# Writing out the order of the first up pairs, and three other buffers for the last pair's totals

## The chip, the cores and the metric

One NeuronCore of a Trainium2 chip runs the whole layer as one launch. The metric is the device time in microseconds (us) of one execution; the number compared is the median of several runs. Engines are named as in the profile: PE (TensorE matmul), PEld (its weight loads), DVE (VectorE), ACT (ScalarE), POOL (GpSimd), SP (the queue that issues most DMAs).

## The reference, cut to what matters

A hybrid layer on x (1024 tokens by 1024 channels, float32): a state-space branch and an attention branch, merged by gates, then a gated MLP with a causal convolution of three taps along the tokens. The change lies in the MLP:

```python
h = rms_norm(x, norm_ffn_g[i])
u = causal_depthwise_conv(h @ w_up[i], conv_ffn_w[i], conv_ffn_b[i])
u_gate, u_val = jnp.split(u, 2, axis=-1)
x = x + (jax.nn.silu(u_gate) * u_val) @ w_down[i]
```

`w_up` is 1024 by 5632, so `u_gate` and `u_val` have 2816 channels each, 22 tiles of 128.

## The kernel before, in words

**Numbers.** Each float32 operand is split into a high half (a cast on ACT to a rounded format) and a low half (operand minus high half, a subtraction on DVE or POOL). A product of two 128-wide blocks is three matmuls of 128x128 by 128x512, high by high, high by low, low by high (lines L175, L176, L177).

**Up pairs.** The MLP's first product goes over 22 pairs `q` (`q.j` = 0 to 21; q0, q1, q2, q3 are the first four). A pair is one gate tile and one value tile of `w_up` (raw weights `q.r1` and `q.r2`, tiles `ur1` and `ur2`) times the 1024 tokens. As a 2x2 block product (two halves of the 1024 inputs, two halves of the tokens) it is done in seven block products instead of eight, with sums of weights (`w_sums`) and sums of activations (the `job`s "t1" to "t4" and "22", whose high and low halves are tiles `tq` and `h`). A block product is 12 matmuls. PE does them per pair as: `p12` (two block products, banks `q.x` and `q.y`), `p5` (bank `q.z`), `p6` (onto `q.x`), `p3` (onto `q.z`), `p7` (onto `q.x`), `p4` (onto `q.x`). Operands: `q.a` (w_first), `q.b` (w_second), `q.c` (w_third), `q.d` (w_fourth), `q.e` for p4(q0). p5(q3) means p5 of the fourth pair.

**Between the products** a bank is copied out by ACT (L1315 `c11`, L1322 `p5`, L1327 `p6`, L1367 `c21`) or added into a row by DVE (L1316, L1338 `c22`, L1353 `p3`, L1473 and L1477 for the first two pairs). The next product onto the same bank has to wait for that reader. The rows `ug` (gate) and `uv` (value) hold 1024 tokens and two zeros in front. A conv half takes a new bank: one ACT start (L1346) and two DVE steps (L1348). `gate` puts the silu of both halves into `uc`; `value_half` multiplies the value conv into it on DVE (L1371); `totals` writes sums of two pairs to DRAM (`f_d`) for the down product, which has the same 7-of-8 form.

**Buffers.** PSUM has 8 banks: two named `lin`, six named `dps` (`bank6`), shared by products and convs, given out as the program is recorded; a new holder waits for the last reader of the old one. `wraw` has two buffers, `lt` three, `ur1` and `ur2` two each.

**Order.** PE's instructions are chained in the order of the code everywhere. The other engines (not SP) are chained in code order only in three stretches, one of them from `strict` to `strict_end`, which in the kernel before ends right behind p4(q1). Outside these a scheduler places instructions. From `ordered` on (the last pair, `totals` of both last pairs on DVE, first operands of the down product, L1559 and L1564) code order holds again.

Of the kernel before, what the change touches and what calls it, by code (L numbers as in the profile page):

```python
# [72 lines left out]
def tile_hybrid_layer(ctx: ExitStack, tc: tile.TileContext, x, cols, cons, w_main, w_small, w_uq, w_ukv,  # L73
# [105 lines left out]
    def act_tile():  # L179
        return hp.tile([P, 2, 512], F32R, name="h")  # L180
# [941 lines left out]
    def w_raw(q, name=None):  # L1122
        q.r1 = up.tile([P, KD, P], F32, name="ur1", bufs=2)
        q.r2 = up.tile([P, KD, P], F32, name="ur2", bufs=2)
        for raw, j in ((q.r1, q.j), (q.r2, FFT + q.j)):
            nc.sync.dma_start(out=raw, in_=w_up[j])
            if name:
                behind(name)

    def w_tiles(n, wide=True):  # L1130
        if n < 2:
            return wpool.tile([P, KD, P], F32R, name="whi"), wpool.tile([P, KD, P], F32R, name="wlo")
        k = KD if wide else 4
        return (ux[0].tile([P, k, P], F32R, name=f"xhi{n}", bufs=1), ux[0].tile([P, k, P], F32R, name=f"xlo{n}", bufs=1))

    def w_split(raw, hl, eng):
        hi, lo = [t[:, 0:raw.shape[1], :].rearrange(flat) for t in hl]
        r = raw.rearrange(flat)
        S.copy(hi, r)  # L1139
        eng.tensor_sub(lo, r, hi.bitcast(F32))  # L1140
        return hl

    def w_first(q):
        q.a = w_split(q.r1, w_tiles(0), G)

    def w_sums(q, t=None):
        q.s = t or up.tile([P, KD, P], F32, name="us", bufs=1)
        G.tensor_tensor(q.s[:, 0:4, :], q.r2[:, 0:4, :], q.r2[:, 4:8, :], op=ALU.add)
        G.tensor_tensor(q.s[:, 4:8, :], q.s[:, 0:4, :], q.r1[:, 0:4, :], op=ALU.subtract)
        G.tensor_tensor(q.r2[:, 0:4, :], q.r1[:, 0:4, :], q.r2[:, 0:4, :], op=ALU.subtract)  # L1150
        G.tensor_tensor(q.r1[:, 4:8, :], q.r1[:, 4:8, :], q.s[:, 4:8, :], op=ALU.subtract)
# [17 lines left out]
    with tc.tile_pool(name="ep", bufs=2) as ep:  # L1169
# [159 lines left out]
        def p7(q):  # L1329
            drain([product(q.x, q.c, 0, "t3", False, True)])  # L1330
# [6 lines left out]
            value_row(q)  # L1337
            V.tensor_tensor(q.uv[:, 514:1026], q.x, q.q, op=ALU.add)  # L1338

        def conv(q, kind, u, half):  # L1340

            c = bank6()
            ct = kind * FFT + q.j
            cw = CG_FW + 3 * ct
            n = half * 512
            S.activation(c, u[:, n + 2:n + 514], AF.Identity, bias=col(CG_FB + ct), scale=col(cw + 2))  # L1346
            for k in range(2):
                V.scalar_tensor_tensor(c, u[:, n + k:n + k + 512], col(cw + k), c, op0=ALU.mult, op1=ALU.add)  # L1348
            return c

        def p3(q):
            drain([product(q.z, q.d, 0, "22", False, True)])
            V.tensor_tensor(q.ug[:, 514:1026], q.z, q.s2, op=ALU.add)  # L1353

        def gate_tile_(q):
            q.gate = ux[0].tile([P, T], F32, name="uc0", bufs=2)

        def gate(q):
            gate_tile_(q)
            for half in range(2):  # L1360
                S.activation(q.gate[:, hs_(half)], conv(q, 0, q.ug, half), AF.Silu)
# [16 lines left out]
        def totals(q, eng=G):  # L1378
            kp = q.j // 2
            t0, t1 = q.gate[:, 0:512], q.gate[:, 512:1024]  # L1380

            def total(n, a, b, op, t):
                eng.tensor_tensor(t, a, b, op=op)  # L1383
# [34 lines left out]
        def low(left=0):  # L1418
            while len(late) > left:
                lo, v, hi, name, i, t = late.pop(0)  # L1420
                V.tensor_sub(lo, v, hi.bitcast(F32))
                BQ[name][i] = t

        def job(name, i, v, t, minuend=None, subtrahend=None):

            if minuend is not None:
                V.tensor_tensor(v, minuend, subtrahend, op=ALU.subtract)
            hi, lo = [t[:, n, :].rearrange("p (i c) -> p i c", c=P) for n in range(2)]
            S.copy(hi, v)
# [43 lines left out]
        V.tensor_tensor(q0.q, q0.x, q0.q, op=ALU.add)  # L1473
# [34 lines left out]
    def first_operands(k):
        a, b = [up.tile([P, KD, P], F32, name=f"ur{n}", bufs=2).rearrange(rows) for n in (1, 2)]
        nc.sync.dma_start(out=a, in_=f_d[k][:, 0:2, :].rearrange(rows))  # L1510
        nc.sync.dma_start(out=b, in_=w_down[0, k].rearrange(rows))
        first.append((split_pair(a, act_tile), split_pair(b, tq)))

    def raw_w(count=[0]):
        count[0] += 1
        return wpool.tile([P, 2, 512], F32, name=("whi", "wlo")[count[0] % 2])

    for j in range(3, FFT):
        nx = Pair()
        nx.j = j  # L1520
        w_raw(nx)
        w_first(nx)
        p5(q)
        if j == 3:
# [24 lines left out]
        before, q = q, nx
# [271 lines left out]
```

## Time and profile before

| | |
|---|---|
| runs, not profiled | 2189.15, 2190.39, 2189.43 us; median 2189.43 |
| profiled execution | 2194.85 us; its span (first to last instruction) 2192.9 us |
| mean granted PE clock | 0.996 |
| PE busy | 2144.1 us of the span |
| pairs 0 to 3 | p7(q0) starts at 1558.37, p12(q4) at 1617.28 us |
| a load of 512 KB (q2's value weights) | issued at 1560.59, used by POOL at 1564.15 us |
| last pair's end, start of the down product | PE's wait at 1984.7 to 1988.0 us |

Times in the prediction's rows are microseconds from the start of the span. A timeline row gives start, duration, engine, line, operation, what it writes from what, shape, count, and in brackets how long the engine stood idle before it and who released it. A row with x2 or x4 is a run of like instructions in one, so the step to the next row is the price of the run.

### The profile page before, as it was taken

The page shows a single profiled execution, that of the slowest core. Times are in us where ns is not written, and L with a number is a line of the kernel's source. Part 1 is how long each engine was busy: PE and PEld are TensorE (multiplying, and loading weights), DVE is VectorE, ACT ScalarE, POOL GpSimd, SP SyncE. Part 2 cuts the span into 40 slices and gives each one's busy share as a digit, 9 for nine tenths or more (in the row PEclk, how much of TensorE's full clock was granted, in tenths as well). Part 3 has the DMA queues.
Part 4 walks back from the last instruction along what each step waited for, and adds up shares of the span by engine and source line. Part 5 has one row for each costly group of instructions (what it writes and reads, how often), then busy time and mean ns, then how long its engine had stood idle before and what let it go on. Part 6 is the DMA issues. An engine that isn't in the chain of part 4 may idle for free. (4 is left out here: it accounts for less than half of the span.)

```text
span 2192.9 us, 30400 instructions
## 1 busy us (share of the span) xinstructions
PE 2144.1 (98%) x10844; PEld 1712.9 (78%) x10844; DVE 1447.2 (66%) x2609; ACT 1063.8 (49%) x2032; POOL 889.8 (41%) x1005
## 2 busy tenths in 40 slices
PE   8999999999999999999999999999899999999999
PEld 6877776777777887778877787887678888887887
DVE  4466656576664469898877745545766666676773
ACT  5445454555454446665654424324655545554341
POOL 2244424432443237665545311003277777840000
PEclk9999999999999999999999999999999999999999
DMA  4221111111112324554366566552133222248752
GB/s 148 69 69 46 40 54 62 49 38 55 64 44 78 108 77 148 180 168 154 116 220 208 173 215 222 162 174 97 61 107 106 102 101 96 106 156 305 268 188 82
DMA packets 121768, 269.50 MB, mean 123 GB/s; under 512 B 13520, under 2 KB 25744, under 8 KB 121616
## 3 DMA queue, kind: packets, MB, share of 16 engines
q1 hardware_dynamic: 105600, 214.99, 29.3%
q0 software_dynamic: 14528, 49.29, 6.8%
q10 hardware_dynamic: 1488, 3.28, 0.4%
q8 instruction: 85, 1.39, 0.3%
q14 instruction: 67, 0.55, 0.1%
HBM read 201.97 MB, written 65.54 MB: 122 GB/s over the span
## 5 line engine op out<-in xcount | busy, mean ns | idle before, releaser
L175 PE MATMUL lin<-h,whi 128*128 128x512 f32 x1440 | 591.6, 411 | 0.7 <-DVE lt L330 0.6
L177 PE MATMUL lin<-h,wlo 128*128 128x512 f32 x1440 | 563.7, 391 | 0.1
L176 PE MATMUL lin<-h,whi 128*128 128x512 f32 x1440 | 562.5, 391 | 0.0
L175 PEld LDWEIGHTS lin<-h,whi 128*128 128x128 f32 x1440 | 270.7, 188 | 83.5 <-issue 33.8
L177 PEld LDWEIGHTS lin<-h,wlo 128*128 128x128 f32 x1440 | 270.3, 188 | 60.0 <-DVE wlo L154 0.5
L176 PEld LDWEIGHTS lin<-h,whi 128*128 128x128 f32 x1440 | 271.4, 189 | 53.0 <-issue 6.7
L153 ACT CAST whi<-wraw 128x512 fp32r<-128x512 f32 x232 | 140.9, 619 | 256.8 <-PE lin L176 112.7
L154 POOL TENSOR_TENSOR wlo<-wraw,whi 128x512 fp32r<-128x512 f32 x134 | 193.3, 1460 | 169.0 <-ACT whi L153 165.1
L664 POOL TENSOR_TENSOR acc<-acc,e 128x512 f32<-128x512 f32 (+3 forms) x80 | 78.9, 987 | 246.0 <-ACT e L659 224.3
L659 ACT ACTIVATE e<-s 128x512 f32<-128x512 f32 (+1 forms) x192 | 93.4, 492 | 152.1 <-DVE s L657 131.1
L1140 DVE TENSOR_TENSOR xlo<-ur,xhi 128x512 fp32r<-128x512 f32 (+1 forms) x41 | 82.9, 2022 | 61.4 <-ACT xhi L1139 61.4
L154 DVE TENSOR_TENSOR wlo<-wraw,whi 128x512 fp32r<-128x512 f32 x98 | 69.9, 725 | 73.0 <-ACT whi L153 72.7
L850 ACT ACTIVATE seg<-abc,acum 128x128 f32<-128x128 f32 x256 | 80.1, 389 | 46.9 <-PE yp L891 37.3
L176 PE MATMUL dps<-tq,h 128*128 128x512 f32 x242 | 96.6, 399 | 3.1 <-DVE tq L1564 3.1
L177 PE MATMUL dps<-tq,h 128*128 128x512 f32 x242 | 96.4, 398 | 0.0
L175 PE MATMUL dps<-tq,h 128*128 128x512 f32 x242 | 96.3, 398 | 0.0
L812 DVE SCALAR_TENSOR_TENSOR xg<-craw,cl,xg 128x1024 f32<-128x1024 f32 x48 | 73.8, 1537 | 27.4 <-ACT xg L810 26.9
L664 DVE TENSOR_TENSOR acc<-acc,e 128x512 f32<-128x512 f32 (+3 forms) x80 | 55.3, 691 | 37.8 <-ACT e L659 37.2
L670 PE MATMUL pv<-e,vt 128*64 128x512 f32 (+3 forms) x384 | 72.9, 499 | 0.0
L629 DVE CUSTOM_DVE_ANT_0 s<-s,negw 128x128 f32<-128x128 f32 (+3 forms) x128 | 62.3, 495 | 13.5 <-PE s L627 13.3
L175 PE MATMUL s<-qh,kh 97*128 97x512 f32 (+1 forms) x192 | 68.6, 357 | 1.3 <-ACT qh L644 0.9
L1216 POOL DMA_DIRECT2D mt<-m_d x16 | 8.6, 540 | 145.6 <-DVE gt L1225 96.6
(628 smaller groups left out, 5133.4 us busy)
## 6 DMA issues: line engine op xcount, KB each, us to landing
wraw<-in_w_main SPq DMA_DIRECT2D x112, 256.0 KB
ur<-in_w_up SPq DMA_DIRECT2D x44, 512.0 KB
abc<-ac_d POOLq DMA_DIRECT2D x32, 512.0 KB, 5.4
wraw<-in_w_ssd SPq DMA_DIRECT2D x64, 256.0 KB
ar<-f_d SPq DMA_DIRECT2D x32, 512.0 KB
f_d<-wraw POOLq DMA_DIRECT2D x33, 256.0 KB, 2.4
g_d<-lt SPq DMA_DIRECT2D x32, 256.0 KB
z_d<-lt SPq DMA_DIRECT2D x32, 256.0 KB
```

The lines of the kernel that those rows point to most:

```text
L153: S.copy(hi, raw)
L154: (eng or V).tensor_sub(lo, raw, hi.bitcast(F32))
L175: PE.matmul(ps, lhsT=ah, rhs=bh, start=first, stop=False, **more)
L176: PE.matmul(ps, lhsT=ah, rhs=bl, start=False, stop=False, **more)
L177: PE.matmul(ps, lhsT=al, rhs=bh, start=False, stop=last, **more)
L629: V.tensor_tensor_reduce(ps[:, 0:w], ps[:, 0:w], negw[:, 512 - w:512], 1.0, 2 * NEG, ALU.add, ALU.max, nm[:, j, i:i + 1])
L659: S.activation(e[:, c0:512], ps[:, 0:w], AF.Exp)
L664: (V if hd else G).tensor_tensor(accs[hd][:, c0:512], accs[hd][:, c0:512], e[:, c0:512], op=ALU.add)
L670: PE.matmul(pv[hd * 64:(hd + 1) * 64, c0:512], lhsT=vt[:, j, hd * 64:(hd + 1) * 64], rhs=es[hd][:, c0:512], start=first, stop=last)
L812: V.scalar_tensor_tensor(c, raw[:, k:k + T], col(cw + k), c, op0=ALU.mult, op1=ALU.add)
L850: S.activation(seg[:, hd, :], abc[:, hd, :], AF.Relu, bias=acum[:, c, 8 * g + hd:8 * g + hd + 1], scale=-1.0)
L1140: eng.tensor_sub(lo, r, hi.bitcast(F32))
```

## The change

Three things. First, `strict_end` moves: code order now holds on all engines through p4 of the third pair (q2), and that stretch of code is written out by hand instead of by conditions `j == 3` in the loop. Second, within it: two of the "t3" jobs go ahead of p5's bank copy; the additions that read p7(q0)'s and p7(q1)'s bank come right behind those products; `w_sums(q2)` is done on DVE instead of POOL, its last two sums later; q2's raw gate weights go into q0's tile in two DMAs; the copy of q2's first bank (`s1`) and the casts of q2's and q3's weights come ahead of the silus; both gate halves of a pair get their ACT start and bank before either is finished (`conv_begin`, `conv_end`, `gate_both`). Third, the three totals of the last pair (`q.j == 21`) are formed in `lt` buffers instead of `wraw`.

The diff's core (names of new helpers; `successor` is `w_raw` and `w_first` of a new pair):

```diff
-        def conv(q, kind, u, half):
+        def conv_begin(q, kind, u, half):
             c = bank6()
...
+            return c, u, n, cw
+
+        def conv_end(c, u, n, cw):
             for k in range(2):
                 V.scalar_tensor_tensor(c, u[:, n + k:n + k + 512], col(cw + k), c, op0=ALU.mult, op1=ALU.add)
             return c
...
+        def gate_both(q):
+            gate_tile_(q)
+            begun = [conv_begin(q, 0, q.ug, half) for half in range(2)]
+            for half, c in enumerate(begun):
+                S.activation(q.gate[:, hs_(half)], conv_end(*c), AF.Silu)
...
             def raw():
+                if q.j == FFT - 1:
+                    return lt.tile([P, 512], F32, name="lt")
                 return wpool.tile([P, 512], F32, name="wraw", bufs=2)
...
-        for q in (q0, q1):
-
-            p5(q, q.ug[:, 514:1026])
-        for i in range(4):
+        def job_t3(i):
             job("t3", i, b[3, i], tq(), b[4, i], b[3, i])
+
+        for i in range(2):
+            job_t3(i)
+        p5(q0, q0.ug[:, 514:1026])
+        job_t3(2)
+        p5(q1, q1.ug[:, 514:1026])
+        job_t3(3)
...
         p6(q0)
-        q1.c = w_split(q1.r2, w_tiles(0), V)
-        for i in range(2):
-            job("t4", i, b[2, i], tq(), b[2, i], b[1, i])
+        q1.c = w_tiles(0)
+        S.copy(q1.c[0].rearrange(flat), q1.r2.rearrange(flat))
+        job_t4(0)
+        V.tensor_sub(q1.c[1].rearrange(flat), q1.r2.rearrange(flat), q1.c[0].rearrange(flat).bitcast(F32))
         p6(q1)
-        for i in range(2, 4):
-            job("t4", i, b[2, i], tq(), b[2, i], b[1, i])
+        for i in range(1, 3):
+            job_t4(i)
+        p7(q0)
+        V.tensor_tensor(q0.q, q0.x, q0.q, op=ALU.add)
+        job_t4(3)
         low()
         q0.e = w_split(q0.r2[:, 4:8, :], w_tiles(1), V)
-        p7(q0)
-        V.tensor_tensor(q0.q, q0.x, q0.q, op=ALU.add)
...
+    s1 = lt.tile([P, 512], F32, name="lt")
+    S.copy(s1, q2.x)
+    p3(q0)
     w_second(q2, V)
-    w_third(q2)
-    p3(q0)
-    gate(q0)
+    gate_tile_(q0)
+    begun = [conv_begin(q0, 0, q0.ug, half) for half in range(2)]
+    w_sums_last(q2, V)
     p3(q1)
     w_fourth(q2)
...
+    q, nx = q2, q3
+    p5(q)
+    gate_row(q)
+    V.tensor_tensor(q.ug[:, 2:514], q.y, s1, op=ALU.add)
+    value_half(q0, 0)
+    p6(q)
+    w_sums(nx)
+    p3(q)
+    value_half(q0, 1)
+    totals(q0)
+    w_second(nx)
+    p7(q)
+    c22(q)
+    gate_both(q1)
+    gate_row(nx)
+    drain([p12(nx)])
+    value(q1)
+    c11(nx)
+    w_fourth(nx)
+    p4(q)
+    c21(q)
+    gate_both(q)
+    w_third(nx)
+    strict_end = len(nc.cur_bb.bb.instructions)
+    value(q)
```

In the three places below, the line numbers are each kernel's own; the changed kernel's L1349, L1354, L1326, L1319 and L1398 are before's L1346, L1348, L1322, L1315 and L1383.

ACT behind p4(q1), before: `dps_14887` is q2's first bank (`q2.x`), `dps_15298` is p5(q2)'s bank, `uc0_15262` is q0's gate, `dps_15263` and `dps_15268` are its conv halves, `xhi2` and `xhi3` the high halves of q2.c and q2.d, `whi_15294` that of q3.a.

```order
L1361 ACT_TABLE_LOAD
L1361 ACTIVATE uc0_15262<-dps_15263 128x512
L1139 CAST whi_15241<-us_15228 128x1024
L1139 CAST xhi2_15245<-ur2_15225 128x1024
L1346 ACTIVATE dps_15268<-ug_14861,cl_80 128x512
L1139 CAST xhi3_15286<-ur1_15224 128x512
L1139 CAST whi_15294<-ur1_15290 128x1024
L1346 ACTIVATE dps_15337<-uv_15233,cl_80 128x512
L1346 ACTIVATE dps_15342<-uv_15233,cl_80 128x512
L1322 COPY lt_15311<-dps_15298 128x512
L1361 ACTIVATE uc0_15262<-dps_15268 128x512
L1315 COPY lt_15315<-dps_14887 128x512
```

The same place now; `lt_15239` is the copy of q2's first bank, `dps_15300` p5(q2)'s bank, `uc0_15258` q0's gate, `whi_15289` q3.a.

```order
L1521 COPY lt_15239<-dps_14887 128x512
L1139 CAST whi_15254<-us_15228 128x1024
L1349 ACTIVATE dps_15259<-ug_14861,cl_80 128x512
L1349 ACTIVATE dps_15261<-ug_14861,cl_80 128x512
L1139 CAST xhi3_15278<-ur1_13668 128x512
L1530 CAST xhi2_15282<-ur2_15224 128x1024
L1139 CAST whi_15289<-ur1_15285 128x1024
L1536 ACT_TABLE_LOAD
L1536 ACTIVATE uc0_15258<-dps_15259 128x512
L1536 ACTIVATE uc0_15258<-dps_15261 128x512
L1326 COPY lt_15313<-dps_15300 128x512
```

The first bank's copy went from last to first, the table load from first to behind the casts, and the copy of p5(q2)'s bank stands behind both silus.

ACT a little later, q1's gate and value, before: `uc0_15351` is q1's gate, `dps_15352` and `dps_15357` its gate convs, `dps_15381` and `dps_15386` its value convs.

```order
L1346 ACTIVATE dps_15352<-ug_14863,cl_80 128x512
L1346 ACTIVATE dps_15357<-ug_14863,cl_80 128x512
L1139 CAST whi_15364<-us_15318 128x1024
L1327 COPY lt_15335<-dps_14887 128x512
L1346 ACTIVATE dps_15381<-uv_15237,cl_80 128x512
L1346 ACTIVATE dps_15386<-uv_15237,cl_80 128x512
L1139 CAST xhi3_15413<-ur1_15290 128x512
L1361 ACTIVATE uc0_15351<-dps_15352 128x512
L1346 ACTIVATE dps_15403<-ug_15313,cl_80 128x512
L1361 ACTIVATE uc0_15351<-dps_15357 128x512
```

The same now, with `uc0_15383`, gate convs `dps_15384` and `dps_15386`, value convs `dps_15422` and `dps_15427`.

```order
L1349 ACTIVATE dps_15384<-ug_14863,cl_80 128x512
L1349 ACTIVATE dps_15386<-ug_14863,cl_80 128x512
L1376 ACTIVATE uc0_15383<-dps_15384 128x512
L1376 ACTIVATE uc0_15383<-dps_15386 128x512
L1349 ACTIVATE dps_15422<-uv_15235,cl_80 128x512
L1349 ACTIVATE dps_15427<-uv_15235,cl_80 128x512
L1319 COPY lt_15443<-lin_15396 128x512
```

Before, the value convs were started ahead of the silus; now they stand behind the second silu, which needs DVE's last gate conv step. The next holder of `dps_15427`'s bank is p5(q3)'s `dps_15500`.

DVE at the end, before: the five operations of `totals` for the two last pairs (`ud` for pair 20, three `wraw` for pair 21, the last one in place) and the first low halves of the down product behind them.

```order
L1383 TENSOR_TENSOR ud<-uc_18183 128x512
L1383 TENSOR_TENSOR wraw<-uc_18183,uc_18259 128x512
L1383 TENSOR_TENSOR wraw<-ud,uc_18259 128x512
L1383 TENSOR_TENSOR wraw<-uc_18259 128x512
L1383 TENSOR_TENSOR wraw<-wraw,ud 128x512
L1564 TENSOR_TENSOR h<-ur_18414,h 128x1024
L1564 TENSOR_TENSOR tq<-ur_18415,tq 128x1024
```

And now:

```order
L1398 TENSOR_TENSOR ud<-uc_18183 128x512
L1398 TENSOR_TENSOR lt<-uc_18183,uc_18259 128x512
L1398 TENSOR_TENSOR lt<-ud,uc_18259 128x512
L1398 TENSOR_TENSOR lt<-uc_18259 128x512
L1398 TENSOR_TENSOR lt<-lt,ud 128x512
L1618 TENSOR_TENSOR h<-ur_18414,h 128x1024
L1618 TENSOR_TENSOR tq<-ur_18415,tq 128x1024
```

The order is the same; only the buffers written differ.

More of the change, by code (lines that the diff above doesn't have):

```diff
@@ L1144, in w_first, with w_sums, w_sums_last @@
         q.a = w_split(q.r1, w_tiles(0), G)
-    def w_sums(q, t=None):
+    def w_sums(q, t=None, eng=G):
         q.s = t or up.tile([P, KD, P], F32, name="us", bufs=1)
[L1148 to L1151, printed above, removed]
+        eng.tensor_tensor(q.s[:, 0:4, :], q.r2[:, 0:4, :], q.r2[:, 4:8, :], op=ALU.add)
+        eng.tensor_tensor(q.s[:, 4:8, :], q.s[:, 0:4, :], q.r1[:, 0:4, :], op=ALU.subtract)
+        if eng is G:
+            w_sums_last(q, eng)
+    def w_sums_last(q, eng):
+        eng.tensor_tensor(q.r2[:, 0:4, :], q.r1[:, 0:4, :], q.r2[:, 0:4, :], op=ALU.subtract)
+        eng.tensor_tensor(q.r1[:, 4:8, :], q.r1[:, 4:8, :], q.s[:, 4:8, :], op=ALU.subtract)
     def w_second(q, eng=None):
@@ L1349, in conv @@
             return c
+        def conv(q, kind, u, half):
+            return conv_end(*conv_begin(q, kind, u, half))
         def p3(q):
@@ L1434, in tq, with job_t4 @@
             return tp.tile([P, 2, 512], F32R, name="tq")
+        def job_t4(i):
+            job("t4", i, b[2, i], tq(), b[2, i], b[1, i])
         for i in range(4):
@@ L1463, in tile_hybrid_layer @@
         p6(q0)
-        q1.c = w_split(q1.r2, w_tiles(0), V)
-        for i in range(2):
-            job("t4", i, b[2, i], tq(), b[2, i], b[1, i])
+        q1.c = w_tiles(0)
+        S.copy(q1.c[0].rearrange(flat), q1.r2.rearrange(flat))
+        job_t4(0)
+        V.tensor_sub(q1.c[1].rearrange(flat), q1.r2.rearrange(flat), q1.c[0].rearrange(flat).bitcast(F32))
         p6(q1)
-        for i in range(2, 4):
-            job("t4", i, b[2, i], tq(), b[2, i], b[1, i])
+        for i in range(1, 3):
[3 more added lines that the diff above has]
+        job_t4(3)
         low()
         q0.e = w_split(q0.r2[:, 4:8, :], w_tiles(1), V)
-        p7(q0)
-        V.tensor_tensor(q0.q, q0.x, q0.q, op=ALU.add)
-        for i in range(2):
-            job("22", i, b[4, i], act_tile())
         p7(q1)
         V.tensor_tensor(q1.q, q1.x, q1.q, op=ALU.add)
-        for i in range(2, 4):
+        for i in range(4):
             job("22", i, b[4, i], act_tile())
@@ L1484, in tile_hybrid_layer @@
         p4(q)
-    strict_end = len(nc.cur_bb.bb.instructions)
-    w_raw(q2)
-    w_sums(q2)
+    q2.r1 = q0.r1
+    q2.r2 = up.tile([P, KD, P], F32, name="ur2", bufs=2)
+    nc.sync.dma_start(out=q2.r2, in_=w_up[FFT + q2.j])
+    for n in range(2):
+        nc.sync.dma_start(out=q2.r1[:, 4 * n:4 * n + 4, :], in_=w_up[q2.j][:, 4 * n:4 * n + 4, :])
+    w_sums(q2, None, V)
     for q in (q0, q1):
@@ L1491, in tile_hybrid_layer @@
         c21(q)
+    s1 = lt.tile([P, 512], F32, name="lt")
+    S.copy(s1, q2.x)
+    p3(q0)
     w_second(q2, V)
-    w_third(q2)
-    p3(q0)
-    gate(q0)
+    gate_tile_(q0)
+    begun = [conv_begin(q0, 0, q0.ug, half) for half in range(2)]
+    w_sums_last(q2, V)
     p3(q1)
     w_fourth(q2)
-    q = q2
+    q2.c = w_tiles(2)
+    S.copy(q2.c[0].rearrange(flat), q2.r2.rearrange(flat))
+    q3 = Pair()
+    q3.j = 3
+    w_raw(q3)
+    w_first(q3)
+    for half, c in enumerate(begun):
+        S.activation(q0.gate[:, hs_(half)], conv_end(*c), AF.Silu)
+    V.tensor_sub(q2.c[1].rearrange(flat), q2.r2.rearrange(flat), q2.c[0].rearrange(flat).bitcast(F32))
     rows = "p a b -> p (a b)"
@@ L1506, in split_pair @@
         return hl
[L1508 to L1512, printed above, removed]
     def raw_w(count=[0]):
@@ L1516, in raw_w, with successor @@
         return wpool.tile([P, 2, 512], F32, name=("whi", "wlo")[count[0] % 2])
-    for j in range(3, FFT):
+    def successor(j):
         nx = Pair()
@@ L1522, in tile_hybrid_layer @@
         w_first(nx)
+        return nx
+    q, nx = q2, q3
[23 more added lines that the diff above has]
+    value(q)
+    q = nx
+    for j in range(4, FFT):
+        nx = successor(j)
         p5(q)
-        if j == 3:
-            gate_row(q)
-            c11(q)
         w_sums(nx)
         p6(q)
-        if j == 3:
-            value(q0)
-            gate(q1)
         gate_row(nx)
@@ L1535, in tile_hybrid_layer @@
         p3(q)
-        if j == 3:
-            value(q1)
         gate(q)
```

## The prediction

> **What bounds the kernel now.** First the busy time by engine, then PE's own waits, then PE's timeline round each wait.
>
> ```profile
> PE 2144.1 (98%) x10844; PEld 1712.9 (78%) x10844; DVE 1447.2 (66%) x2609; ACT 1063.8 (49%) x2032; POOL 889.8 (41%) x1005
> ```
>
> PE (TensorE) is the bound, and the change leaves its instructions and their order as they are. So it can only move PE's idle time. PE's waits (engine, line, releaser: us in total, times, longest) in the part that the diff touches are these five:
>
> ```profile
> PE dps L176 <- DVE tq L1564: 3.1, 1, 3.1
> PE dps L175 <- ACT lt L1315: 3.1, 1, 3.1
> PE lin L175 <- DVE ug L1473: 2.0, 1, 2.0
> PE lin L175 <- ACT lt L1327: 1.5, 1, 1.5
> PE dps L175 <- DVE uv L1338: 1.3, 1, 1.3
> ```
>
> Four lie between 1558 and 1618 us (pairs 0 to 3), the first at 1985 us, where the down projection starts. PE's timeline (start, duration, then what it waited for):
>
> ```profile
> 1558.37 0.50 PE L175 MATMUL lin<-tq,us 128*128 128x512 f32 x1
> ...
> 1562.92 0.50 PE L175 MATMUL lin<-tq,whi 128*128 128x512 f32 x1 [1.50 <-ACT lt L1327]
> ...
> 1567.97 0.48 PE L175 MATMUL lin<-tq,whi 128*128 128x512 f32 x1 [2.00 <-DVE ug L1473]
> ...
> 1585.23 0.79 PE L175 MATMUL dps<-h,whi 128*128 128x512 f32 x1 [3.09 <-ACT lt L1315]
> ...
> 1591.23 0.39 PE L177 MATMUL dps<-h,xlo 128*128 128x512 f32 x1
> ...
> 1603.26 0.50 PE L175 MATMUL dps<-tq,xhi 128*128 128x512 f32 x1 [1.31 <-DVE uv L1338]
> ...
> 1606.15 0.40 PE L175 MATMUL dps<-tq,whi 128*128 128x512 f32 x1
> ...
> 1617.28 0.39 PE L175 MATMUL lin<-h,whi 128*128 128x512 f32 x1
> ...
> 1984.51 0.40 PE L175 MATMUL dps<-tq,h 128*128 128x512 f32 x1
> 1988.02 0.79 PE L176 MATMUL dps<-tq,h 128*128 128x512 f32 x1 [3.11 <-DVE tq L1564]
> ...
> 1994.02 0.40 PE L175 MATMUL lin<-tq,h 128*128 128x512 f32 x1
> ```
>
> Undisturbed pitch: 1606.15 is the start of p5(q3), 1617.28 that of p12(q4), 48 matmuls later: 0.232 us each. From p7(q0) at 1558.37 to 1617.28 PE does 204 matmuls, 47.3 us at that pitch, in 58.9: **11.6 us are lost**, more than the four waits (7.9). Each wait costs some 0.2 more round the restart, and after the long one the clock falls. The windows (granted clock third from the end) show it:
>
> ```profile
> 1565.00:1570.00 5.00, 3.00 (x14) 2.15 (x13) 5.00 (x8) 2.57 (x5) 0.47 (x1) 1.00 0.32 102
> 1585.00:1590.00 5.00, 4.77 (x11) 3.80 (x12) 5.00 (x9) 1.65 (x3) 4.49 (x5) 0.50 0.43 151
> 1985.00:1990.00 5.00, 1.98 (x5) 1.59 (x6) 5.00 (x5) 0.00 (x0) 0.54 (x1) 0.70 0.33 84
> ```
>
> After 3.09 idle the clock is 0.50, and 14 matmuls (1585.23 to 1591.23) take 6.0 instead of 3.25: 2.75 lost. After 2.00 it stays 1.00. At the end 15 matmuls from 1984.51 to 1994.02 take 9.51 instead of 3.48: **6.0 lost**. At most 17.6 us can be had.
>
> **The last pair's totals.** DVE at that place:
>
> ```profile
> 1979.31 0.69 DVE L1383 TENSOR_TENSOR wraw<-ud,uc 128x512 f32<-128x512 f32 x1
> 1984.28 0.69 DVE L1383 TENSOR_TENSOR wraw<-uc 128x512 f32<-128x512 f32 x1 [4.28 <-DMA f_d<-wraw]
> 1985.00 0.69 DVE L1383 TENSOR_TENSOR wraw<-wraw,ud 128x512 f32<-128x512 f32 x1
> 1985.61 1.22 DVE L1564 TENSOR_TENSOR h<-ur,h 128x1024 fp32r<-128x1024 f32 x1
> 1986.75 1.22 DVE L1564 TENSOR_TENSOR tq<-ur,tq 128x1024 fp32r<-128x1024 f32 x1
> ```
>
> The third total waits 4.28 us until the first has been written out of its buffer (two buffers `wraw`, three totals). With three `lt` buffers, whose last readers come before the totals in DVE's order, it starts at 1979.9, and the low half that PE wants ends at 1987.97 − 4.36 = 1983.6. PE asks for it at 1984.51 + 0.23 = 1984.7, so 1.1 us of cover is left. Behind it DVE's rows repeat every 1.14, four of them while PE eats 24 matmuls (5.6 us) a step: nothing is late next. The sum takes all 6.0.
>
> **The four early waits.** (1) 1.50: p7(q1) waits for the copy of p6(q1)'s bank, behind two casts of t4 on ACT. Now one t4 cast and a 1024 cast stand ahead, and PE needs the copy only at 1558.37 + 2.8 = 1561.2, 2.7 after p6(q1) ended: gone. (2) 2.00: p4(q0) waits for the addition that reads p7(q0)'s bank. It now comes straight behind p7(q0), so it ends near 1562.0 against 1564.0. What is late next is the low half of q0.e:
>
> ```profile
> 1551.03 1.54 DVE L1348 SCALAR_TENSOR_TENSOR dps<-ug,cl,dps 128x512 f32<-128x512 f32 x2
> 1554.16 0.69 DVE L1421 TENSOR_TENSOR tq<-x,tq 128x512 fp32r<-128x512 f32 x1 [1.59 <-ACT tq L1429]
> ...
> 1566.54 0.68 DVE L1140 TENSOR_TENSOR wlo<-ur,whi 128x512 fp32r<-128x512 f32 x1
> ```
>
> It ended at 1567.2; the two conv steps (1.5) and the 1.6 wait leave the way ahead of it, the addition (0.6) comes in: 1564.7, with smaller waits closed up 1564.5. The third matmul of p4(q0) wants it at 1564.4: **0.2 stays**. (3) 3.09: p6(q2) waits for the copy of q2's first bank (L1315), which stood behind the silus; it is now the first of that group, ten microseconds early: gone with its 2.75. (4) 1.31: p4(q2) waits for c22(q2); c22 now stands ahead of gate(q1): gone.
>
> **What is late instead.** ACT prices: table load and silu, 1024 cast, silus, conv starts. DVE prices: conv pair on one bank, a conv pair with product, a 1024 low half while POOL works.
>
> ```profile
> 1574.42 1.28 ACT L1361 ACT_TABLE_LOAD   x1
> 1575.72 0.60 ACT L1361 ACTIVATE uc<-dps 128x512 f32<-128x512 f32 x1
> ...
> 1601.75 1.04 ACT L1139 CAST whi<-ur 128x1024 fp32r<-128x1024 f32 x1 [1.90 <-PE dps L176]
> 1602.70 1.08 ACT L1361 ACTIVATE uc<-dps 128x512 f32<-128x512 f32 x2
> ...
> 1607.69 1.49 ACT L1346 ACTIVATE dps<-uv,cl 128x512 f32<-128x512 f32 x2
> ```
>
> ```profile
> 1607.21 3.15 DVE L1140 TENSOR_TENSOR xlo<-ur,xhi 128x1024 fp32r<-128x1024 f32 x1 [3.41 <-ACT xhi L1139]
> ...
> 1614.11 1.54 DVE L1348 SCALAR_TENSOR_TENSOR dps<-ug,cl,dps 128x512 f32<-128x512 f32 x2
> 1615.55 0.68 DVE L1353 TENSOR_TENSOR ug<-dps,lt 128x512 f32<-128x512 f32 x1
> ...
> 1973.69 1.54 DVE L1348 SCALAR_TENSOR_TENSOR dps<-uv,cl,dps 128x512 f32<-128x512 f32 x2
> 1975.32 0.69 DVE L1371 TENSOR_TENSOR uc<-uc,dps 128x512 f32<-128x512 f32 x1
> 1975.93 1.54 DVE L1348 SCALAR_TENSOR_TENSOR dps<-uv,cl,dps 128x512 f32<-128x512 f32 x2
> ```
>
> So a step to the next row costs: 512 wide on DVE 0.6, 1024 1.14, conv pair 1.44, pair with product 2.24; on ACT table load 1.3, 1024 cast 0.95, silu 0.5, conv start 0.7. p3(q0) starts at 1558.37 + 48 × 0.232 + 0.2 = 1569.7 and has retired by 1572.6. Then DVE adds its bank (0.6), does q2.b's low half (1.14) and the last two sums (0.6 each): 1575.6. ACT casts q2.d (0.6), q2.c and the next pair's weights (0.95 each), loads the table (1.3), does two silus (1.0) and copies p5(q2)'s bank (0.6): 1581.0. PE reaches p3(q2), which needs that copy, at 1580.8: **0.3 lost** with the restart.
>
> DVE goes on: q2.d's low half to 1576.95, two conv pairs 1579.85, q2.c's low half (1.14 alone, 3.15 beside POOL; I take 1.75, since POOL's cast-splits and sums overlap it only in part) 1581.6, addition 1582.2, value half 1584.5, addition 1585.1, value half 1587.3, c22 1587.9, two conv pairs 1590.8. ACT may only then do the second silu of q1 and behind it start q1's value conv (0.5 + 0.8 with the hand-over): 1592.25. Two value halves follow on DVE: 1596.8. The built program gives p5(q3)'s bank dps_15500 the place of dps_15427, which that last product reads. PE is there at 1558.37 + 156 × 0.232 + 0.5 = 1595.0: **1.9 lost**; bounds 0 and 3.3 (both low halves at 3.15, less what the waits for PE absorb).
>
> After 2.00 the clock stayed up, after 3.09 it cost 2.75: for 1.9, with the 0.3 before it, bounds 0 and 2.75, taken **1.0**. The Trainium skill ("TensorE: Matmul & The Clock Gate", Part 1: the HAM clock gate) has the clock halved after at least one idle window of about 3.4 us; by that the term is 0 and the gain 14.9. The trace does not fully bear it out: 3.09 was enough.
>
> Last, q3.c's low half on DVE: 1596.8, two 512 rows (1.2), six conv steps (4.3), a product (0.6), a conv pair (1.44): 1604.3, plus 1.14 to 3.15; p7(q3) wants it at 1596.9 + 36 × 0.232 + 0.5 = 1605.7. Bounds 0 and 1.8, near the lower: **0.3**.
>
> One more price has two readings. From the table load's start to the silu the trace has 1.30. The Trainium skill ("ScalarE: Activation LUTs", What ACT_TABLE_LOAD costs) counts 1.28 and a drain of about 1.38 besides. Here the load stood behind a copy that had just ended; now it stands behind five ACT instructions in a row. By the page p3(q2) would be 1.4 later, and the value conv behind it 0.9.
>
> The four sums of q2 move from POOL to DVE (4 × 0.6; two of them run while DVE waits for p3(q0) anyway, the other two are in the chain above). The loads: q2's gate weights come in two halves, the first early; q2's second half and q3's go out by 1569.5, behind the low halves of q0.d and q1.d, and are wanted from 1575.0 and 1577.2 on. The load in the table above took 3.6 us from issue to use, so 1.9 and 4.1 us of cover are left. If that went, ACT would stand at q3's cast with the silus and two bank copies queued behind it.
>
> **The sum.** Pairs 0 to 3: 11.6 − 0.2 − 0.3 − 1.9 − 1.0 − 0.3 = 7.9. End: 6.0. Together **13.9 us**. The profiled execution took 2194.85 (span 2192.9), 5.4 more than the median 2189.43 of the runs; its gain is taken off both: 2181.0 and **2175.5**.
>
> **Rivals.** *Nothing new late beyond the 0.2 and 0.3*: 17.1 gained, 2172.3. For it: DVE stood idle 1.59 and 3.41 us at two places of this stretch (rows above). Against: the value conv hangs on the second silu. *The clock stays full*: 14.9, 2174.5. *The table load drains as well*: 0.9 less, 2176.4. *DVE is the new bound*: POOL works beside both low halves: 3.3 + 2.75 + 1.2 + 1.5 for the earlier two lost, 8.8 gained, 2180.6. *The end wait only changes its releaser* (PE needs another low half or load as late): 6.0 less, 2181.5; against it stands the 1.1 of cover. *Slower*: q3's gate load comes late and ACT stands at its cast; each us late beyond 1577.2 is a us at p3(q2). With 2.75 of clock the gain is eaten from 11.2 late on; at 15.6 late the time is 2193.9. Against: the 4.1 of cover. That the order isn't what the change says is ruled out by the built program.
>
> **Chances.** Forecast 0.45, clock full 0.15, table drain 0.10, nothing late 0.10, DVE bound 0.11, end wait stays 0.04, slower 0.05, of which 0.02 falls within 0.2% (4.4 us, about what a measurement of this kernel can tell from no change). So faster 0.95 (all but the last), same 0.02, slower 0.03. The range reaches from the gain of all but the small leftovers, 17.6, to the end wait staying: 2171.8 to 2181.5.
>
> **What would show it.** Right: PE's waits for lt L1315, lt L1327, ug L1473, uv L1338 and tq L1564 are gone; DVE's wait for the DMA of `wraw` too; p12(q4) starts some 8 us earlier after p7(q0); p5(q3) waits about 2 us for the product of q1's second value half. Wrong: a wait above 3 us there with the clock at 0.5 after it, a PE wait at p3(q2) above 1 us, or one left near 1985.

## The result, and the profile after

| | before | after |
|---|---|---|
| median of the runs, us | 2191.89 (6 runs, 2189.15 to 2195.68) | 2179.39 (6 runs, 2177.29 to 2181.82) |
| ratio after to before | | 0.9943, 95% interval 0.9930 to 0.9956 |
| span of the profiled execution, us | 2192.9 | 2177.1 |
| p7(q0) to p12(q4), 204 matmuls, us | 58.91 | 51.34 |
| 15 matmuls at the start of the down product, us | 9.51 | 3.49 |

The medians differ by 12.5 us (9.6 to 15.3 by the interval), against a forecast of 13.9. Of the 15.8 us between the two profiled spans, 7.6 lie in the first stretch and 6.0 in the second. 1.8 come from ahead of p7(q0) and 0.4 from all the rest behind it. Of the 1.8, some 1.6 are not the change's: the clock fell at 1533.04 us in before, behind two short waits, and did not fall in after. In e5, e6, e8 and e9 below, whose code there is that of after, it fell as well.

PE's waits in the changed kernel (engine, line, releaser: total, times, longest), all that are left in the part the diff touches:

```profile
PE dps L175 <- DVE uc L1386: 1.7, 1, 1.7
...
PE lin L177 <- DVE xlo L1140: 1.0, 1, 1.0
...
PE dps L175 <- ACT lt L1326: 0.4, 1, 0.4
```

All five waits of before are gone. Three new ones stand at p5(q3), p7(q3) and p3(q2). PE's timeline of the changed kernel shows them in their places, the first row being the start of p7(q0), the last of the first group p12(q4), and the last two the same 15 matmuls of the down product:

```profile
1556.58 0.40 PE L175 MATMUL lin<-tq,us 128*128 128x512 f32 x1
...
1562.89 0.50 PE L177 MATMUL lin<-tq,wlo 128*128 128x512 f32 x1
...
1579.77 0.50 PE L175 MATMUL dps<-h,xhi 128*128 128x512 f32 x1 [0.42 <-ACT lt L1326]
...
1595.45 0.47 PE L175 MATMUL dps<-tq,whi 128*128 128x512 f32 x1 [1.71 <-DVE uc L1386]
...
1605.52 0.50 PE L177 MATMUL lin<-tq,xlo 128*128 128x512 f32 x1 [1.03 <-DVE xlo L1140]
...
1607.92 0.39 PE L175 MATMUL lin<-h,whi 128*128 128x512 f32 x1
...
1975.14 0.39 PE L175 MATMUL dps<-tq,h 128*128 128x512 f32 x1
...
1978.63 0.40 PE L175 MATMUL lin<-tq,h 128*128 128x512 f32 x1
```

Counted as start minus the start before it minus the pitch of 0.23, the four gaps are 0.2 (at 1562.89), 0.6, 1.9 and 1.2 us. The clock doesn't fall in this stretch (granted clock third from the end), not even behind the 1.71:

```profile
1590.00:1595.00 5.00, 3.75 (x17) 2.77 (x15) 4.00 (x6) 4.61 (x8) 4.88 (x7) 1.00 0.00 0
1595.00:1600.00 5.00, 4.55 (x20) 3.75 (x21) 5.00 (x7) 3.52 (x6) 4.92 (x4) 1.00 0.53 181
```

DVE's timeline at the end of the changed kernel. The third total now starts straight behind the second, into an `lt` buffer, and the low half that PE wants at 1975.37 is done at 1974.23:

```profile
1969.95 0.68 DVE L1398 TENSOR_TENSOR lt<-ud,uc 128x512 f32<-128x512 f32 x1
1970.55 0.68 DVE L1398 TENSOR_TENSOR lt<-uc 128x512 f32<-128x512 f32 x1
...
1973.01 1.22 DVE L1618 TENSOR_TENSOR tq<-ur,tq 128x1024 fp32r<-128x1024 f32 x1
```

### The profile page after: what moved, and what is told of

Same layout as the page of the kernel before. It is cut to its first block, busy times and chain, and to the rows that moved or that the text cites. A ratio compares the mean times of both kernels' runs of the same rounds, so it can differ in the third digit from the quotient of the medians.

```text
span 2177.1 us, 30390 instructions
## 1 busy us (share of the span) xinstructions
PE 2136.6 (98%) x10844; PEld 1708.5 (78%) x10844; DVE 1445.6 (66%) x2613; ACT 1063.4 (49%) x2032; POOL 885.1 (41%) x1001
## 4 chain that ended last, share of the span: by engine, by line
PE 75%; DVE 13%; ACT 5%; DMA 4%; issue 2%; POOL 1%; SPq 0%; ACTq 0%; DVEq 0%; POOLq 0%
PE lin L175 14%; PE lin L177 14%; PE lin L176 13%; PE dps L176 6%; PE dps L175 6%; PE dps L177 6%; PE pv L670 3%; PE s L175 2%; PE s L176 2%; PE s L177 2%; DVE xg L812 1%; PE s L627 1%; DMA wraw<-in_w_ssd 1%; PE yp L891 1%; PE s L610 1%
```

## The experiments

Spans of single executions differ by several us through stalls far from the change (p7(q0) starts between 1553.45 and 1562.09 us in the profiles), so most runs are read by "the stretch", the time from p7(q0) to p12(q4) in their own profile. Undisturbed it would be 47.3 us. Each run without a ratio is one execution. The "chain theory" in the expectations is that DVE's row of conv steps, products and low halves sets when PE may go on, so that a wait removed at one place comes back at the next.

### The two gains apart

e1 takes the kernel before and gives it only this:

```diff
             def raw():
+                if q.j == FFT - 1:
+                    return lt.tile([P, 512], F32, name="lt")
```

> The kernel before with only the last pair's three totals in lt buffers. Theory (two gains that have nothing to do with each other): the waits of pairs 0 to 3 stay (1.5, 2.0, 3.1, 1.3 us) and the 58.9 us from p7(q0) to p12(q4) with them, the wait of 3.1 us for tq L1564 and the slow matmuls behind it go, 15 matmuls there take 3.5 instead of 9.5: 6.0 us faster, ratio 0.9973. Rival (the end is early enough only because pairs 0 to 3 moved too): PE keeps a wait of over 1 us near 1985, gain under 3 us, ratio over 0.9987.

e2 is the changed kernel without those two lines.

> The changed kernel with the last pair's totals in wraw again. Theory: the stretch from p7(q0) to p12(q4) takes the 51.3 us of the changed kernel, the end has its 3.1 us of waiting and its slow matmuls back: 7.6 us faster than before, ratio 0.9965. Rival (what moved earlier also shifts the last pair's writes, so the end's stall goes by itself): 10 to 13.6 us faster, ratio 0.994 to 0.9955.

| | median, us | ratio to before | stretch | wait near the down product |
|---|---|---|---|---|
| e1 | 2186.46 (before: 2191.25) | 0.9978 (0.9968 to 0.9988) | 56.87 | none |
| e2 | 2185.96 (before: 2191.25) | 0.9976 (0.9965 to 0.9987) | 51.35 | 3.5 |

The two gains are separate, and both rivals fall: e1 has no wait left at the end and its 15 matmuls there take 3.48, e2 keeps the wait, and its 15 matmuls take 9.98. PE's wait there in e2:

```profile
PE dps L176 <- DVE tq L1616: 3.5, 1, 3.5
```

By the runs e1 gives 4.8 us and e2 5.3 where 6.0 and 7.6 were expected. Both expected ratios lie within the intervals, that of e2 at the very end of its. e1's timeline and window show a likely reason for the smaller gains. It still has the wait for the copy of q2's first bank, 3.10 us as before, but this time the clock stays at 1.00:

```profile
1588.91 0.50 PE L175 MATMUL dps<-h,whi 128*128 128x512 f32 x1 [3.10 <-ACT lt L1315]
```

```profile
1585.00:1590.00 5.00, 1.90 (x9) 1.26 (x8) 5.00 (x8) 4.45 (x7) 4.92 (x4) 1.00 0.41 136
```

Its stretch is 2.0 shorter than that of before: the 2.75 lost to the clock are not lost, and the wait for uv L1338 grows by 0.7 in return. So what the reordering wins against one execution is 5.5 us (56.87 − 51.34) or 7.6, as the clock stays up in it or falls. At the end it would be 3.3 (the gap up to 1988.02 in before, less the pitch) instead of 6.0 if the clock stayed up. No run shows that: both waits seen there, in before and in e2, halved it.

### Are the leftover waits costs of their own?

e3 records p5(q3) ahead of `value(q2)`, so that it gets the bank of q1's first value half.

```diff
+    p5(nx)
     value(q)
     q = nx
 
     for j in range(4, FFT):
         nx = successor(j)
-        p5(q)
+        if j > 4:
+            p5(q)
```

> The changed kernel with p5(q3) recorded ahead of value(q2), so that its bank is the one of q1's first value half, free 1.5 us before the second: PE's wait of 1.7 us at p5(q3) goes. Chain theory (DVE's run of conv steps and products up to q3.c's low half ends at the same time as before, whatever PE does): p7(q3) then waits about 3 us instead of 1.0, and the stretch from p7(q0) to p12(q4) stays within 0.5 us of the changed kernel's 51.3. Rival (each of PE's waits is a cost of its own, as my sum had it): the stretch falls by 1.9 to 49.5 and p7(q3) still waits 1.0.

PE's timeline of e3 at p7(q3), and the window there:

```profile
1605.48 0.50 PE L175 MATMUL lin<-tq,xhi 128*128 128x512 f32 x1 [1.43 <-ACT xhi L1139]
1605.81 0.40 PE L176 MATMUL lin<-tq,xhi 128*128 128x512 f32 x1
1607.45 0.66 PE L177 MATMUL lin<-tq,xlo 128*128 128x512 f32 x1 [1.24 <-DVE xlo L1140]
1607.90 0.63 PE L175 MATMUL lin<-tq,xhi 128*128 128x512 f32 x1
```

```profile
1605.00:1610.00 5.00, 3.28 (x8) 2.33 (x9) 4.90 (x7) 1.73 (x4) 4.59 (x4) 0.76 0.53 186
```

The wait at p5(q3) is gone and comes back whole at p7(q3), 1.43 for the cast of q3.c and 1.24 for its low half. The stretch is 52.93. Eight matmuls behind the second wait are 0.2 slower each, since the clock is halved there, and without these 1.6 it would be 51.3, as the chain theory has it. An earlier PE only waits longer at the next place that hangs on DVE.

e4 takes the other end, q3.c's cast and low half ahead of q2's gate convs.

```diff
     c21(q)
-    gate_both(q)
     w_third(nx)
+    gate_both(q)
```

> The changed kernel with q3.c's cast and low half ahead of q2's gate convs instead of behind them. Chain theory: the low half ends near 1598, PE asks for it at 1604.3, so p7(q3)'s wait of 1.0 goes and the stretch falls by 1.2 to 50.1; p5(q3) still waits 1.7. Rival (the convs of q2 pushed back by 2 us make another bank late): a new wait of 1 us or more at p12(q4) or p7(q3), the stretch 51 or more.

p7(q3)'s wait goes and p5(q3) still waits 1.72, as expected. But a new wait of 1.76 comes up, not at either place named but at p3(q3), which needs the copy of p5(q3)'s bank:

```profile
1600.79 0.50 PE L175 MATMUL dps<-h,xhi 128*128 128x512 f32 x1 [1.76 <-ACT lt L1326]
```

The stretch is 52.17, 0.8 worse. e9 shortens DVE's chain itself. In the changed kernel DVE stands idle there until ACT has started q1's value conv:

```profile
1590.86 1.55 DVE L1354 SCALAR_TENSOR_TENSOR dps<-uv,cl,dps 128x512 f32<-128x512 f32 x2 [1.41 <-ACT dps L1349]
```

e9 gives that start its place ahead of the silus:

```diff
-    gate_both(q1)
+    gate_tile_(q1)
+    begun = [conv_begin(q1, 0, q1.ug, half) for half in range(2)]
+    vals = [conv_begin(q1, 1, q1.uv, half) for half in range(2)]
+    for half, c in enumerate(begun):
+        S.activation(q1.gate[:, hs_(half)], conv_end(*c), AF.Silu)
     gate_row(nx)
     drain([p12(nx)])
-    value(q1)
+    for half, c in enumerate(vals):
+        g = q1.gate[:, hs_(half)]
+        V.tensor_tensor(g, g, conv_end(*c), op=ALU.mult)
+    totals(q1)
```

> The changed kernel with the ACT starts of q1's two value convs ahead of q1's silus instead of behind them. Chain theory: DVE's idle 1.41 us behind q1's gate convs goes, all of it lies on the chain: p5(q3)'s wait falls from 1.7 to about 0.3, p7(q3)'s stays near 1.0, stretch 49.9. Rival (DVE's rate or another engine sets it): stretch 51 or more with the wait at p5(q3) or p7(q3) as long as now.

PE's timeline of e9 at p5(q3) and at p3(q3):

```profile
1595.68 0.50 PE L175 MATMUL dps<-tq,whi 128*128 128x512 f32 x1 [0.26 <-DVE uc L1579]
...
1602.93 0.50 PE L175 MATMUL dps<-h,xhi 128*128 128x512 f32 x1 [1.43 <-ACT lt L1326]
```

p5(q3)'s wait falls to 0.26, so the start behind the second silu was what held it. But the wait of 1.0 at p7(q3) does not stay as expected. It is replaced by 1.43 at p3(q3), again for ACT's copy, and the stretch is 50.39 instead of 49.9. ACT's timeline of e9 shows why: the copy stands behind q2's first silu, and that waits for POOL's total to let go of its buffer.

```profile
1601.81 0.60 ACT L1376 ACTIVATE uc<-dps 128x512 f32<-128x512 f32 x1 [2.20 <-POOL wraw L1398]
1602.30 0.58 ACT L1326 COPY lt<-dps 128x512 f32<-128x512 f32 x1
```

### Which part of the change removed which wait

e5 puts the copy of q2's first bank behind q0's silus again.

```diff
-    s1 = lt.tile([P, 512], F32, name="lt")
-    S.copy(s1, q2.x)
     p3(q0)
...
     for half, c in enumerate(begun):
         S.activation(q0.gate[:, hs_(half)], conv_end(*c), AF.Silu)
+    s1 = lt.tile([P, 512], F32, name="lt")
+    S.copy(s1, q2.x)
```

> The changed kernel with the copy of q2's first bank behind q0's silus again, as before the change. Chain theory: the copy ends near 1579.7 on the changed kernel's clock, PE waits some 3.1 us at p6(q2), p3(q2)'s wait of 0.4 goes, DVE's c22(q2) and all behind it on DVE come 2.5 later, p5(q3) and p7(q3) wait as long as now: stretch from p7(q0) to p12(q4) 51.3 + 2.5 = 53.8, and 2.7 more if the clock is halved after the wait, which the phase of the wait decides. Rival (the later waits are slack that takes up an earlier delay): p5(q3) and p7(q3) no longer wait, stretch 51.3 to 52.

PE's timeline of e5 at p6(q2):

```profile
1583.20 0.50 PE L175 MATMUL dps<-h,whi 128*128 128x512 f32 x1 [3.16 <-ACT lt L1536]
```

The clock stays at 1.00, p3(q2)'s wait is gone, and the stretch is 53.92, as the theory had it (53.8). The copy's place is worth 2.6 us plus whatever the clock takes. The later waits (1.5 and 0.8) give only 0.4 back.

e6 puts the addition that reads p7(q0)'s bank back behind the last t4 job.

```diff
-        p7(q0)
-        V.tensor_tensor(q0.q, q0.x, q0.q, op=ALU.add)
         job_t4(3)
         low()
         q0.e = w_split(q0.r2[:, 4:8, :], w_tiles(1), V)
+        p7(q0)
+        V.tensor_tensor(q0.q, q0.x, q0.q, op=ALU.add)
```

> The changed kernel with the addition that reads p7(q0)'s bank behind the last t4 job and q0.e's low half again. Theory: the addition ends near 1563.4 instead of 1560.2, p4(q0) waits 1.0 to 1.3 us for it in place of the 0.2 for the low half, and as DVE waits for p3(q0) later all moves along: stretch 52.3 to 52.6. Rival (the whole wait of 2.0 hung on this place alone): wait of 2.0, stretch 53.3 or more.

The stretch is 51.46. The place of this addition is worth 0.1 us, so both expectations fail. The addition and q0.e's low half only change places: the addition ends at 1562.44 and the low half at 1561.83, against 1560.26 and 1562.83 in the changed kernel, where p7(q0) starts at the same time. e7 tries the t3 jobs instead:

```diff
-        for i in range(2):
-            job_t3(i)
         p5(q0, q0.ug[:, 514:1026])
-        job_t3(2)
         p5(q1, q1.ug[:, 514:1026])
-        job_t3(3)
+        for i in range(4):
+            job_t3(i)
```

> The changed kernel with the t3 jobs behind both of p5's bank copies again. Theory (this place, not the addition's, is what ended the wait of 2.0 at p4(q0)): the first t3 casts wait on ACT behind the copy of p5(q1)'s bank until about 1551.8 on the changed kernel's clock, DVE stands idle 2 to 3 us there as it did before (1.59), q0.e's low half ends 1.0 to 1.5 later, and p4(q0) waits that much more: stretch from p7(q0) to p12(q4) 52.3 to 52.8. Rival (DVE's idle 1.04 us a little later takes it up): stretch within 0.3 of 51.3.

The stretch is 52.82, and p4(q0) waits 1.14, about as expected. DVE's timeline of e7 shows where it starts, eleven microseconds earlier: the low half of the first t3 job waits for a cast that stands behind p5(q1)'s copy.

```profile
1554.33 0.69 DVE L1438 TENSOR_TENSOR tq<-x,tq 128x512 fp32r<-128x512 f32 x1 [3.05 <-ACT tq L1446]
```

e8 gives the four sums of q2 back to POOL.

```diff
-    w_sums(q2, None, V)
+    w_sums(q2)
...
-    w_sums_last(q2, V)
```

> The changed kernel with the four sums of q2's weights on POOL again. Chain theory: POOL, idle there, does them in 5 to 7 us from about 1567.5; DVE is rid of 1.2 us ahead of q0's gate convs and ACT casts q2.d 1 to 2 us earlier, so p3(q2)'s wait of 0.4 goes and p5(q3)'s wait falls by up to 1.2: stretch 50.1 to 51. Rival (the move to DVE was needed): the sums come late on POOL, PE waits over 0.5 us at p5(q2) or p3(q2), stretch over 51.5.

The stretch is 55.05, 3.7 worse, and the wait is at none of the places expected. The first load arrives so early that POOL starts at 1560. POOL's and DVE's timelines of e8, and PE's:

```profile
1560.05 1.50 POOL L1148 TENSOR_TENSOR us<-ur 128x512 f32<-128x512 f32 x1 [48.38 <-DMA ur<-in_w_up]
1561.62 1.61 POOL L1149 TENSOR_TENSOR us<-us,ur 128x512 f32<-128x512 f32 x1
1563.19 1.70 POOL L1154 TENSOR_TENSOR ur<-ur,ur 128x512 f32<-128x512 f32 x1
```

```profile
1560.31 3.47 DVE L1438 TENSOR_TENSOR tq<-x,tq 128x512 fp32r<-128x512 f32 x2
1563.70 1.75 DVE L1140 TENSOR_TENSOR wlo<-ur,whi 128x512 fp32r<-128x512 f32 x1
```

```profile
1565.50 0.79 PE L177 MATMUL lin<-tq,wlo 128*128 128x512 f32 x1 [3.15 <-DVE wlo L1140]
```

In the changed kernel the same two rows of DVE take 1.46 and 0.68, with POOL at rest:

```profile
1560.78 1.46 DVE L1438 TENSOR_TENSOR tq<-x,tq 128x512 fp32r<-128x512 f32 x2
1562.15 0.68 DVE L1140 TENSOR_TENSOR wlo<-ur,whi 128x512 fp32r<-128x512 f32 x1
```

POOL's three sums make DVE's three low halves 3.1 us longer, and the low half of q0.e comes that much later to p4(q0), with half a clock behind it (0.66 in the window 1565 to 1570), which is some 1.3 of the 3.7.

### A version without the leftovers

e10 joins e9 with four more moves of bank copies and low halves, that of e4 among them (the edit of e9 isn't shown again):

```diff
+        q0.e = w_split(q0.r2[:, 4:8, :], w_tiles(1), V)
         job_t4(3)
         low()
-        q0.e = w_split(q0.r2[:, 4:8, :], w_tiles(1), V)
...
+    p5(q2)
     for half, c in enumerate(begun):
         S.activation(q0.gate[:, hs_(half)], conv_end(*c), AF.Silu)
...
     q, nx = q2, q3
-    p5(q)
...
     c21(q)
-    gate_both(q)
     w_third(nx)
+    gate_tile_(q)
+    begun = [conv_begin(q, 0, q.ug, half) for half in range(2)]
+    p5(nx)
+    p6(nx)
+    for half, c in enumerate(begun):
+        S.activation(q.gate[:, hs_(half)], conv_end(*c), AF.Silu)
...
     for j in range(4, FFT):
         nx = successor(j)
-        p5(q)
+        if j > 4:
+            p5(q)
         w_sums(nx)
-        p6(q)
+        if j > 4:
+            p6(q)
```

> The changed kernel with five edits: q1's value convs started ahead of its silus; q3.c's cast and low half ahead of q2's gate convs; p5(q3) and p6(q3), with their bank copies, recorded ahead of q2's silus (so p5(q3) gets a bank that is free); p5(q2)'s copy ahead of q0's silus; q0.e's low half ahead of the last t4 job. Theory: the waits of 0.2, 0.4, 1.7 and 1.0 us go, and the new ones seen one at a time (1.4 to 1.8 at p3(q3) for ACT's copy) don't come, since that copy no longer stands behind a silu: stretch 47.5 to 48.5, about 3 us under the changed kernel's 51.3. Rival (DVE is short of time over the whole stretch): a wait of 1.5 us or more comes up at p12(q4) or at p4(q3) just behind it, stretch to the 260th matmul over 62.5 (changed kernel 64.2).

The stretch is 47.52, as expected, with one gap of 0.3 left (p3(q3) behind the copy of p5(q3)'s bank). It was then timed, with the changed kernel beside it on the same chip.

> The kernel of e10, timed beside the changed kernel on the same chip. If the 3.8 us less in the stretch are all of it: a median 3.8 us under the changed kernel's, ratio to before some 0.0017 under the changed kernel's. Rival (PE's earlier arrival is lost again further on, or in stalls elsewhere): less than 2 us between the medians.

> The changed kernel itself, as the other side of that comparison: ratio to before 0.993 to 0.9956 as measured first; the stretch from p7(q0) to p12(q4) 51.3 again, with the waits of 0.4, 1.7 and 1.0 us.

| | median, us | ratio to before (2193.45) | stretch |
|---|---|---|---|
| e11, the kernel of e10 | 2176.93 | 0.9917 (0.9904 to 0.9931) | 47.54 |
| e12, the changed kernel | 2180.01 | 0.9930 (0.9915 to 0.9946) | 51.39 |

PE's timeline of e11, the start of p7(q0) and of p12(q4):

```profile
1558.10 0.40 PE L175 MATMUL lin<-tq,us 128*128 128x512 f32 x1
...
1605.64 0.39 PE L175 MATMUL lin<-h,whi 128*128 128x512 f32 x1
```

The 3.8 us in the stretch are there in both profiles of this kernel, and they aren't lost again further on: from p12(q4) to the end it is 569.2 us in e11 and 569.3 in e12. The profiled span of e11 (2174.8) is 0.7 longer than that of e12 (2174.1) all the same, because its p7(q0) starts 4.65 later, ahead of all that e10's edit touches. The medians differ by 3.1 us, but the two intervals overlap, so by the runs alone this last step is likely and not settled.

## Why the prediction held, step by step

**The forecast.** 2175.5 was 2189.43 − 13.9. The median came out 3.9 higher: 2.5 because six runs of before have the median 2191.89, and 1.4 because the gain is 12.5.

**The last pair's totals** (6.0): 6.0 in the profile, and the cover of 1.1 us is there to the tenth (1975.37 − 1974.23). But 2.7 of it is the halved clock. The sum took both halved clocks of one profiled execution as lost in every run, and e1 shows that the clock does not fall behind every such wait. That is a likely reason why the runs gained 12.5 and not 13.9, though 13.9 lies within their interval.

**The four early waits.** All went. Of the reasons given for (2), the 2.00 at p4(q0), two were weighed wrongly. "It now comes straight behind p7(q0), so it ends near 1562.0" came true (1560.26, as far behind p7(q0) as forecast), but the place is worth 0.1 (e6). What counts of the reasons given is that "the 1.6 wait" leaves the way, that is, the t3 jobs' place ahead of p5's copies (1.5, e7). And "The four sums of q2 move from POOL to DVE" was booked as a cost alone. In the changed kernel this move is worth 3.7 (e8), since POOL would otherwise work beside the very low halves that p4(q0) waits for. The trace of before showed the effect in a smaller size, 0.9: beside one POOL sum, two low halves of DVE took 2.39 instead of 1.46.

```profile
1564.15 1.32 POOL L1148 TENSOR_TENSOR us<-ur 128x512 f32<-128x512 f32 x1 [50.22 <-DMA ur<-in_w_up]
```

```profile
1564.23 2.39 DVE L1421 TENSOR_TENSOR tq<-x,tq 128x512 fp32r<-128x512 f32 x2
```

**What is late instead.**

| | forecast, us | profile, us |
|---|---|---|
| p4(q0), low half of q0.e | 0.2 | 0.2 |
| p3(q2), copy behind table load and silus | 0.3 | 0.6 |
| p5(q3), q1's second value product | 1.9 | 1.9 |
| clock behind it | 1.0 | 0 |
| p7(q3), low half of q3.c | 0.3 | 1.2 |
| gain of the stretch | 7.9 | 7.6 |

The sum is right and two terms are not: 1.0 too much for the clock stands against 0.9 too little at p7(q3) and 0.3 at p3(q2). That the total fits so well is in part luck. Of "for 1.9, with the 0.3 before it, bounds 0 and 2.75" the lower bound held, where 1.0 was taken. The Trainium skill ("TensorE: Matmul & The Clock Gate", Part 1) would have had it so. "Last, q3.c's low half … near the lower: 0.3": the low half of q3.d ahead of it took 1.72 beside POOL where the step counted one 512 row of 0.6, q3.c's own took 2.13, and PE, not slowed, came earlier. DVE's timeline of the changed kernel, and POOL's rows beside it:

```profile
1595.83 1.72 DVE L1140 TENSOR_TENSOR xlo<-ur,xhi 128x512 fp32r<-128x512 f32 x1
...
1603.33 2.13 DVE L1140 TENSOR_TENSOR xlo<-ur,xhi 128x1024 fp32r<-128x1024 f32 x1
```

```profile
1594.60 2.39 POOL L1140 TENSOR_TENSOR wlo<-ur,whi 128x1024 fp32r<-128x1024 f32 x1
...
1604.45 2.16 POOL L1398 TENSOR_TENSOR wraw<-wraw,ud 128x512 f32<-128x512 f32 x1
```

The two errors belong together. e3 shows that time won at p5(q3) is waited out at p7(q3), so the terms should have been taken as one end of DVE's chain and not added. By the same argument a slower clock behind p5(q3) would have shortened the wait at p7(q3); no run shows that case.

**The table load.** The load starts at 1576.86, 0.02 behind a cast that ended at 1576.84, and the silu 1.29 later. The drain that the Trainium skill ("ScalarE: Activation LUTs", What ACT_TABLE_LOAD costs) counts besides does not show, and that rival falls. ACT's timeline of the changed kernel:

```profile
1575.80 1.04 ACT L1139 CAST whi<-ur 128x1024 fp32r<-128x1024 f32 x1
1576.86 1.28 ACT L1536 ACT_TABLE_LOAD   x1
1578.15 1.09 ACT L1536 ACTIVATE uc<-dps 128x512 f32<-128x512 f32 x2
```

Of the other rivals, "nothing late" (11.1 for the stretch) and "DVE is the new bound" (2.8) are far from the 7.6 and out, as are the end wait and q3's load: ACT casts q3's weights at 1575.80 without a wait. "The clock stays full" is half right: the clock did, and the larger terms at p7(q3) and p3(q2) took the gain.

## What to carry to other kernels

Leftover waits of one engine that hang on the same chain of another are one cost: remove the first alone and it turns up at the next (e3), so look for the end of the chain and for what holds it up (e9), and clear every place on it together (e10). An operation moved off an engine can be worth more than its own time if it slowed the rows of another engine that PE waits for, so look for what ran beside the slow rows before booking a move as a cost (e8). A small ACT copy that frees a bank should not stand behind work that waits for something else (e5, e9).

## What the runs showed of the hardware

**The clock after a wait is not a matter of its length alone.** Waits of 3.09, 3.11, 3.15 and 3.50 us (before, twice; e8; e2) halved the clock, waits of 3.10 and 3.16 (e1, e5) did not, and in e3 1.43 and 1.24 with two matmuls between them did. The Trainium skill ("TensorE: Matmul & The Clock Gate", Part 1) has a free-running window of about 3.4 us. The traces agree: within each profile the clock falls and comes back only at steps of 3.413 us. In before it falls at 1533.04, at 1584.24 (15 steps on) and at 1987.01 (118 more). Where a wait lies in these steps explains the difference. The windows of before and of e1, cut at their steps (PE's busy time second, granted clock third from the end):

```profile
1580.83:1584.24 3.41, 1.32 (x6) 0.74 (x4) 3.41 (x5) 3.31 (x6) 3.33 (x3) 1.00 0.45 143
1584.24:1591.07 6.83, 5.84 (x14) 4.58 (x15) 6.83 (x12) 3.09 (x5) 5.25 (x5) 0.50 0.35 121
```

```profile
1584.08:1587.49 3.41, 1.73 (x8) 1.08 (x6) 3.41 (x5) 3.15 (x5) 3.25 (x3) 1.00 0.33 105
1587.49:1590.90 3.41, 1.99 (x9) 1.65 (x10) 3.41 (x6) 2.68 (x5) 3.41 (x3) 1.00 0.51 192
```

In before one step holds most of the wait, PE is busy in it for 1.32 of 3.41 us, and the clock is 0.50 in the next two. In e1 the end of a step cuts a wait as long, PE is busy for 1.73 and 1.99, and the clock stays. The other waits fit: 1.31 (before, at the end), 0.92 (e3), 0.72 (e2) and 0.70 (e8) fell, 1.71 (e5) and 1.76 (the changed kernel behind its 1.71) stayed. Over the 14 profiles, the half clock followed all 26 steps with PE busy for at most 0.43 of the step, and none with over 0.65. Between these both happen, so the busy share as the profile has it is not the whole rule. The Trainium skill's condition, on the same page, of a whole idle window is too strict for these waits. Part of the runs' spread (2189.15 to 2195.68 for before) may be of this kind: in before the clock also fell from 1533.04 to 1536.46 us, and in after only at 1141.43 to 1144.84 and at the very end, both far from the change.

**POOL beside DVE.** Two low halves of 512 on DVE took 3.47 us with POOL's sums running and 1.46 without, and one took 1.75 against 0.68. The Trainium skill ("SBUF — State Buffer", SBUF: two separate sides) has DVE and POOL take turns at a shared port for whole instructions when DVE reads two operands from SBUF and POOL reads there too. The rows agree: the additional 2.0 and 1.1 us are about one POOL sum (1.50 to 1.70) or less per low half.
